# A fused transformer block on one core: the recurrence's projections token-major, merge blocks between its steps, modulation pieces spread

## The chip, the core and the metric

The kernel runs on one core of one Trainium2 chip. The metric is device time in microseconds (us) of one execution. Before the change three runs gave a median of 1801.65 us (1800.70 to 1803.32).

The engines are named as in the profile: PE is TensorE (matmuls; PEld its weight loads), ACT is ScalarE, DVE is VectorE, POOL is GpSimd and SP is SyncE, which issues the DMAs.

## What is computed

One block with 256 tokens (T) of width 2048 (D), batch 1, in fp32. Shapes and helpers are cut here to what the change touches:

```python
mod = silu(c) @ ada_w + ada_b                      # 2048 -> 6 x 2048: shifts, scales, gates
h = rmsnorm(x, norm1_g) * (1 + sc1) + sh1
z = h @ w_in                                       # 2048 -> 13360 columns
q, kc, vc, ks, vs, kw, vw, g_nsa, lx, ly, ga, gb = split(z)
o_a = nsa_attention(q, kc, vc, ks, vs, kw, vw, g_nsa, ...)   # 16 heads, 4 groups; kc, vc are compressed
u = causal_dwconv(lx, conv_w, conv_b)              # 4 taps over the tokens
r = sigmoid(blockdiag(u, w_a) + b_a);  i = sigmoid(blockdiag(u, w_i) + b_i)
log_a = 8 * r * log_sigmoid(lam)
hs = scan over tokens:  h_t = exp(log_a) h_(t-1) + sqrt(-expm1(2 log_a)) * (i * u)
o_b = gelu(ly) * hs
merged = sigmoid(ga) * (o_a @ proj_a) + sigmoid(gb) * (o_b @ proj_b)
x = x + g1 * (merged @ w_out)
h = rmsnorm(x, norm2_g) * (1 + sc2) + sh2
x = x + g2 * conv_glu_ffn(h, w_up, conv_w, conv_b, w_down)
return rmsnorm(x, final_g)
```

## The kernel before

**Weights and products.** Every weight matrix streams through once, in pieces of 1 MB (`stage`, L97: a tile `raw` of 128x2048, four buffers, loaded by SP's queue). A piece is worked on in two halves of 128x1024. `split` (L107, L108) makes of each half a rounded part `hi` by a copy on ScalarE and the rest `lo` by a subtraction on VectorE (three buffers each). The activations stand in the same two parts next to each other. A product takes three matmuls: hi by high part, hi by low part, lo by high part. All product outputs come from one pool of four PSUM banks (`bank`, name P).

**Two forms of product.** `dense_pair1` (L172 to L190) is feature-major: the weights are the stationary operand, 128 features come out on the partitions, and each matmul moves 256 columns (the tokens); one bank holds two feature tiles. `dense_tok` (L192 to L223) is token-major: the activations are stationary, 128 tokens come out on the partitions, and each matmul moves 512 columns (features); a block needs two banks, one for each half of the tokens. A half of weights is 12 matmuls in this form.

**Modulation pieces.** Most of `ada_w` does not pass through TensorE: `ada_piece` (L232 to L235) loads 1 MB and lets VectorE multiply and sum it into one column (L234). `filler(n)` (L487 to L493) runs the next n of 64 such pieces; the code calls it between blocks of other work. 48 pieces run ahead of the feed-forward network (FFN), the last 16 in it.

**Stages in order of time.** Norm, modulation and the input projection in four parts over the contraction (to about 230 us); its last part with the compression of kc and vc (`gather`, `compress`, to about 296 us); then eight attention units `attention(g, t)` woven into blocks of the input projection (L601 to L672). In the lx stage (L680 to L691) eight `dense_pair1` blocks give lx, with an attention unit and `filler(2)` behind each. The recurrence (L693 to L742) goes over four blocks `bt` of 512 features: the convolution on VectorE into u, two kinds of gate matmuls (banks lru_r and lru_i; the lru_i banks are those of attention's tp and oT), Sigmoid, Tanh, Exp and Sqrt on ScalarE, four scans on VectorE, then two `dense_pair1` blocks of ly whose GELU (L736) is written over u, times the scan's result, into oB (L740). ScalarE must load a table before a function of another set; `tbl(...)` keeps these functions in written order. The merge (L745 to L779) goes over four blocks n of 512 columns with two sides s (proj_a by oA, proj_b by oB): a gate block (n = 0 was computed earlier and lies in `mq`; its Sigmoid, L761, has been moved ahead into the attention), Sigmoid, product, multiply, add, transpose. Then the output projection and the FFN.

**What sets the order.** The kernel is written in the Tile framework. Each engine runs its instructions in one fixed order, which the framework's scheduler makes from the code by a model of the times; so an instruction can stand ahead of one that was written earlier, if nothing it needs is missing in the model. `high_priority` in `split` moves the hi and lo of the next weights ahead. Semaphores between engines keep the data right.

The recurrence's last step, L732 to L742, in short:

```python
for h in range(2):
    pl = dense_pair1([w_lru[8 + pr, k] for k in range(2)], h1r)
    tbl(A.activation(gl, pl..., AF.Gelu_apprx_tanh))
    V.tensor_tensor(gl, gl, iu[:, 2 * h:2 * h + 2], op=ALU.mult)
    ...
    filler(2 if pr % 4 == 0 else 0)
```

## Time and profile before

| | |
|---|---|
| Median of three runs | 1801.65 us |
| Profiled execution, its own time | 1802.45 us |
| Its span in the trace | 1800.3 us |
| PE busy | 1780.1 us, 99% |
| PEld busy | 1553.3 us, 86% |
| DVE busy | 1339.6 us, 74% |
| ACT busy | 871.5 us, 48% |
| POOL busy | 0.2 us |
| Mean granted clock of TensorE | 0.997 of full speed |
| Moved by DMA | 429.51 MB |

"Busy" is the union of an engine's instructions over the span. On TensorE instructions overlap, so their durations add up to more than the busy time; the distance of two starts in the timeline is what one costs. The idle time in front of an instruction is printed with what ended it: "[0.44 <-DVE lo L108]" is an engine that waited 0.44 us for a tile lo that VectorE wrote on line 108. "x8" at the end of a timeline row stands for eight equal instructions in a row.

### The profile page before, as it was taken

The page shows a single profiled execution, that of the slowest core. Times are in us where ns is not written, and L with a number is a line of the kernel's source. Part 1 is how long each engine was busy: PE and PEld are TensorE (multiplying, and loading weights), DVE is VectorE, ACT ScalarE, POOL GpSimd, SP SyncE. Part 2 cuts the span into 40 slices and gives each one's busy share as a digit, 9 for nine tenths or more (in the row PEclk, how much of TensorE's full clock was granted, in tenths as well). Part 3 has the DMA queues.
Part 4 walks back from the last instruction along what each step waited for, and adds up shares of the span by engine and source line. Part 5 has one row for each costly group of instructions (what it writes and reads, how often), then busy time and mean ns, then how long its engine had stood idle before and what let it go on. Part 6 is the DMA issues. An engine that isn't in the chain of part 4 may idle for free.

```text
span 1800.3 us, 25840 instructions
## 1 busy us (share of the span) xinstructions
PE 1780.1 (99%) x10336; PEld 1553.3 (86%) x10336; DVE 1339.6 (74%) x1955; ACT 871.5 (48%) x1185; POOL 0.2 (0%) x4
## 2 busy tenths in 40 slices
PE   8999999999999999999999999999999999999998
PEld 7899998888899888888888998888888888888886
DVE  7899875998788866767666898888555777766555
ACT  5654444655578443434445544444434444444443
POOL 0000000000000000000000000000000000000000
PEclk9999999999999999999999999999999999999999
DMA  9999863666556767777876566787755555555553
GB/s 348 359 333 365 317 231 129 211 214 228 211 179 223 276 239 295 285 288 286 291 274 206 177 234 235 279 283 282 252 190 189 189 192 192 192 190 190 187 192 112
DMA packets 64200, 429.51 MB, mean 239 GB/s; under 512 B 7088, under 2 KB 7376, under 8 KB 15568
## 3 DMA queue, kind: packets, MB, share of 16 engines
q1 hardware_dynamic: 63792, 427.08, 66.8%
q8 instruction: 81, 1.33, 0.3%
q10 hardware_dynamic: 288, 0.79, 0.1%
q14 instruction: 39, 0.32, 0.1%
HBM read 425.72 MB, written 2.11 MB: 238 GB/s over the span
## 4 chain that ended last, share of the span: by engine, by line
PE 94%; DVE 2%; ACT 2%; issue 1%; DMA 1%; DVEq 0%; ACTq 0%
PE P L130 26%; PE P L204 12%; PE P L205 12%; PE P L203 12%; PE P L187 3%; PE P L188 3%; PE P L185 3%; PE P L438 2%; PE P L440 2%; PE P L439 2%; PE P L432 1%; PE P L433 1%; PE P L431 1%; PE P L149 1%; PE P L148 1%; PE P L150 1%
## 5 line engine op out<-in xcount | busy, mean ns | idle before, releaser
L108 DVE TENSOR_TENSOR lo<-raw,hi 128x1024 fp32r<-128x1024 f32 x589 | 718.9, 1223 | 385.2 <-ACT hi L107 384.4
L107 ACT ACTIVATE hi<-raw 128x1024 fp32r<-128x1024 f32 x589 | 623.3, 1061 | 784.4 <-PE P L205 317.0
L130 PE MATMUL P<-h,hi 128*128 128x512 f32 x1344 | 463.9, 394 | 0.0
L130 PE MATMUL P<-h,lo 128*128 128x256 f32 x1344 | 366.4, 278 | 0.0
L130 PEld LDWEIGHTS P<-h,hi 128*128 128x128 f32 x1344 | 249.1, 188 | 54.9
L130 PEld LDWEIGHTS P<-h,lo 128*128 128x128 f32 x1344 | 252.4, 188 | 4.2
L234 DVE SCALAR_TENSOR_TENSOR raw<-raw,crow 128x2048 f32<-128x2048 f32 x64 | 146.4, 2287 | 4.7 <-DMA raw<-ada_w 4.5
L188 PE MATMUL P<-h,lo 128*128 128x256 f32 x512 | 147.7, 289 | 0.6 <-DVE lo L108 0.6
L187 PE MATMUL P<-h,hi 128*128 128x256 f32 x512 | 146.8, 287 | 0.0
L185 PE MATMUL P<-h,hi 128*128 128x256 f32 x512 | 146.7, 287 | 0.0
L438 PE MATMUL P<-h,hi 128*128 128x256 f32 x384 | 108.2, 286 | 0.0
L439 PE MATMUL P<-h,hi 128*128 128x256 f32 x384 | 107.5, 284 | 0.0
L440 PE MATMUL P<-h,lo 128*128 128x256 f32 x384 | 102.0, 283 | 0.0
L188 PEld LDWEIGHTS P<-h,lo 128*128 128x128 f32 x512 | 97.8, 191 | 1.7 <-DVE lo L108 1.4
L187 PEld LDWEIGHTS P<-h,hi 128*128 128x128 f32 x512 | 97.9, 191 | 1.4 <-issue 1.2
L185 PEld LDWEIGHTS P<-h,hi 128*128 128x128 f32 x512 | 97.9, 191 | 1.0 <-issue 0.7
L204 PE MATMUL P<-lo,ua 128*128 128x512 f32 x240 | 93.4, 389 | 0.0
L205 PE MATMUL P<-hi,ua 128*128 128x512 f32 x240 | 93.4, 389 | 0.0
L203 PE MATMUL P<-hi,ua 128*128 128x512 f32 x240 | 83.6, 389 | 0.0
L204 PE MATMUL P<-lo,h 128*128 128x512 f32 x192 | 75.3, 392 | 0.0
L205 PE MATMUL P<-hi,h 128*128 128x512 f32 x192 | 74.9, 390 | 0.0
L438 PEld LDWEIGHTS P<-h,hi 128*128 128x128 f32 x384 | 74.1, 193 | 0.2
(272 smaller groups left out, 3125.0 us busy)
## 6 DMA issues: line engine op xcount, KB each, us to landing
raw<-ada_w SPq DMA_DIRECT2D x96, 1024.0 KB, 5.0
raw<-w_up SPq DMA_DIRECT2D x96, 1024.0 KB, 4.9
raw<-w_down SPq DMA_DIRECT2D x48, 1024.0 KB, 4.9
raw<-w_lru SPq DMA_DIRECT2D x32, 1024.0 KB, 4.9
raw<-w_proj SPq DMA_DIRECT2D x32, 1024.0 KB, 5.0
raw<-w_gates SPq DMA_DIRECT2D x24, 1024.0 KB, 6.5
raw<-w_out SPq DMA_DIRECT2D x16, 1024.0 KB, 5.1
raw<-w_kv SPq DMA_DIRECT2D x24, 512.0 KB, 7.0
```

Of the source, the lines that this page charges most:

```text
L107: A.activation(hi[:, :n], raw[:, lo_col:lo_col + n], AF.Copy)
L108: V.tensor_tensor(lo[:, :n], raw[:, lo_col:lo_col + n], hi[:, :n].bitcast(F32), op=ALU.subtract)
L130: PE.matmul(ps[f][:, 0:256] if w else ps[f], hl[w][:, k * 256 + f * 128:k * 256 + f * 128 + 128], r[:, 0:256] if w else r, start=(kt == 0 ...
L185: PE.matmul(o, hi[:, sl], r[:, 0:256], start=(kt == 0 and f == 0), stop=False, skip_group_check=True)
L187: PE.matmul(o, hi[:, sl], r[:, 256:512], start=False, stop=False, skip_group_check=True)
L188: PE.matmul(o, lo[:, sl], r[:, 0:256], start=False, stop=(kt == n - 1), skip_group_check=True)
L203: PE.matmul(ps[j], xh, hi[:, w], start=(kt == 0), stop=False, skip_group_check=True)
L204: PE.matmul(ps[j], xh, lo[:, w], start=False, stop=False, skip_group_check=True)
L205: PE.matmul(ps[j], xl, hi[:, w], start=False, stop=(kt == n - 1), skip_group_check=True)
L234: V.scalar_tensor_tensor(raw, raw, 1.0, row, op0=ALU.mult, op1=ALU.mult, accum_out=modc[:, c:c + 1])
L438: PE.matmul(o, hi[:, sl], h1[:, kt, 0:256], start=first and f % 2 == 0, stop=False, skip_group_check=True)
L439: PE.matmul(o, hi[:, sl], h1[:, kt, 256:512], start=False, stop=False, skip_group_check=True)
```

## The change

1. **Token-major products for the recurrence.** `dense_pair1` goes. `w_lru` is packed in another layout, and the eight blocks of lx and ly (512 features each) are computed with `dense_tok`. Their output has tokens on the partitions and is turned by the new function `turned`: eight transposes on TensorE into two banks. For lx ScalarE copies the product out of PSUM, the transposes follow, and ScalarE copies them again. For ly the GELU writes the rows into u, the transposes follow, and VectorE multiplies straight from PSUM.
2. **Merge blocks between the steps of the recurrence.** `gates_of`, `open_gates` and `multiply` are the merge's parts as functions. Between the GELU of block bt and its transposes now stands a token-major block of the merge: the product of proj_a for n = 0 behind block 0, the gate block (1, 0) behind block 1, the product (1, 0) behind block 2, the gate block (1, 1) behind block 3. The Sigmoids of gates that wait (`mq` among them) stand in the next block's chain, ahead of its Exp.
3. **Modulation pieces spread.** `filler()` is now called behind each of the seven blocks of the input projection's last part; inside blocks, behind chosen pieces of weights (`fills`); and no longer in groups of two or four behind blocks of the merge. 48 pieces still run ahead of the FFN.
4. **Other slots.** The gathered compressed operands `gat` move from C2, C3 to C4, C5, `cmpb` from C7 to C3; the first of attention's p tiles moves from C3 to a tile xp, of which there is one buffer in place of two; two small tiles share one.

The diff, cut to what is named above:

```diff
-        def dense_pair1(pieces, rhs):
...
-        def dense_tok(pieces, lhs, late=None):
+        def dense_tok(pieces, lhs, late=None, fills=()):
...
+                if ip in fills:
+                    filler()
...
+        def turned(rows):
+            ps = [bank("turn"), bank("turn")]
+            for f in range(4):
+                for j in range(2):
+                    o = (f % 2) * 256 + j * 128
+                    PE.transpose(ps[f // 2][:, o:o + 128], rows[:, j, f * 128:f * 128 + 128], ident)
+            return [p.rearrange("p (f t) -> p f t", f=2) for p in ps]
...
-        gat = [big.tile([128, 16, 4, NCMP], F32, tag="C%d" % (2 + n), name="gat") for n in range(2)]
+        gat = [big.tile([128, 16, 4, NCMP], F32, tag="C%d" % (4 + n), name="gat") for n in range(2)]
...
         for i in range(4):
             whole(i, 3)
+            filler()
...
-        for pr in range(8):
-            pl = dense_pair1([w_lru[pr, k] for k in range(2)], h1r)
-            A.activation(lx[pr // 2][:, 2 * (pr % 2):2 * (pr % 2) + 2],
-                         pl.rearrange("p (f t) -> p f t", f=2), AF.Copy)
-            if units:
-                attention(*units.pop(0))
-            filler(2)
+        for bt in range(4):
+            ps = dense_tok([w_lru[bt, k] for k in range(4)], h1r, fills=(1, 3))
+            rows = lx[bt].rearrange("p (j a) t -> p j (a t)", j=2)
+            for j in range(2):
+                A.activation(rows[:, j], ps[j], AF.Copy)
+            for h, p in enumerate(turned(rows)):
+                A.activation(lx[bt][:, 2 * h:2 * h + 2], p, AF.Copy)
+            for _ in range(2):
+                if units:
+                    attention(*units.pop(0))
...
+        def gates_of(n, s):
+            if n == 0:
+                gated[n, s] = [mq[s][:, j] for j in range(2)]
+                return gated[n, s]
...
+            return dense_tok([w_gates[n - 1, s, k] for k in range(4)], h1r, fills=FILLS)
+
+        def open_gates(n, s, ps):
+            for j in range(2):
+                tbl(A.activation(gated[n, s][j], ps[j], AF.Sigmoid))
+
+        def multiply(n, s):
+            rhs = (lambda kt: oB[kt // 2][:, kt % 2]) if s else (lambda kt: oA[:, kt])
+            ps = dense_tok([w_proj[n, s, k] for k in range(4)], rhs, fills=(0, 1, 3) if s else FILLS)
+            for j in range(2):
+                V.tensor_tensor(gated[n, s][j], ps[j], gated[n, s][j], op=ALU.mult)
+
+        waiting = [(0, s, gates_of(0, s)) for s in range(2)]
...
+            while waiting:
+                open_gates(*waiting.pop(0))
             tbl(A.activation(r, r, AF.Exp, scale=-2.0))
...
-                pl = dense_pair1([w_lru[8 + pr, k] for k in range(2)], h1r)
+            ps = dense_tok([w_lru[4 + bt, k] for k in range(4)], h1r)
+            rows = u.rearrange("p (j a) t -> p j (a t)", j=2)
+            for j in range(2):
+                tbl(A.activation(rows[:, j], ps[j], AF.Gelu_apprx_tanh))
+
+            if bt % 2 == 0:
+                multiply(bt // 2, 0)
+            else:
+                waiting.append((1, bt // 2, gates_of(1, bt // 2)))
+            for h, p in enumerate(turned(rows)):
...
-                V.tensor_tensor(gl, gl, iu[:, 2 * h:2 * h + 2], op=ALU.mult)
+                V.tensor_tensor(gl, p, iu[:, 2 * h:2 * h + 2], op=ALU.mult)
```

**How instructions move.** On TensorE, behind the last attention unit's oT (L666), before: P is a product's bank, h_169 the activations, hi and lo the weights; product matmuls go on in this pattern.

```order
L188 MATMUL P<-h_169,lo 128x256
L666 MATMUL oT<-pT,vN 128x512 x4
L185 MATMUL P<-h_169,hi 128x256
L187 MATMUL P<-h_169,hi 128x256
L188 MATMUL P<-h_169,lo 128x256
```

The same place after (oT is now L660; the product on oA is that with proj_a):

```order
L186 MATMUL P<-hi,oA 128x512
L660 MATMUL oT<-pT,vN 128x512 x4
L736 MATMUL lru_i<-lt,raw 128x256 x2
L184 MATMUL P<-hi,oA 128x512
L185 MATMUL P<-lo,oA 128x512
L736 MATMUL lru_i<-lt,raw 128x256 x2
L186 MATMUL P<-hi,oA 128x512
```

And on TensorE eight matmuls of that product further on, again after:

```order
L186 MATMUL P<-hi,oA 128x512
L734 MATMUL lru_r<-lt,raw 128x256 x2
L736 MATMUL lru_i<-lt,raw 128x256 x2
L734 MATMUL lru_r<-lt,raw 128x256 x2
L736 MATMUL lru_i<-lt,raw 128x256 x2
L215 MATMUL turn<-cols,lt 128x128 x2
L184 MATMUL P<-hi,h_169 128x512
L185 MATMUL P<-lo,h_169 128x512
```

84 of the 96 matmuls of the product with proj_a stand ahead of the last oT; behind it come the other 12, the last four gate matmuls of block 0 and the eight of block 1, and the first two transposes (L215), which read the GELU of block 0. Behind these two stand 18 product matmuls of the next ly block, the other six transposes and 18 more product matmuls, on weights that are split by then. Before, 161 product matmuls stand between the last oT and the next block's first gate matmul on lru_r.

On ScalarE, the end of block 0's gate chain up to its first GELU (lt are the recurrence's tiles: r, iu, tt and u), before:

```order
L107 ACTIVATE hi<-raw 128x1024
L724 ACTIVATE lt<-lt 128x512
L725 ACT_TABLE_LOAD
L725 ACTIVATE lt<-lt 128x1024
L726 ACT_TABLE_LOAD
L726 ACTIVATE lt<-lt 128x1024
L107 ACTIVATE hi<-raw 128x1024 x2
L736 ACT_TABLE_LOAD
L736 ACTIVATE lt<-P 128x512
L107 ACTIVATE hi<-raw 128x1024 x2
L740 ACTIVATE oB<-lt 128x2x256
```

After:

```order
L107 ACTIVATE hi<-raw 128x1024
L744 ACTIVATE lt<-lt 128x512
L704 ACTIVATE mq<-mq 128x512 x4
L107 ACTIVATE hi<-raw 128x1024
L747 ACT_TABLE_LOAD
L747 ACTIVATE lt<-lt 128x1024
L748 ACT_TABLE_LOAD
L748 ACTIVATE lt<-lt 128x1024
L757 ACT_TABLE_LOAD
L757 ACTIVATE lt<-P 128x512 x2
L740 ACT_TABLE_LOAD
L740 ACTIVATE lt<-lru_r,cols 128x256
```

The Sigmoids on mq stand in the chain, and both GELUs (L757) stand between it and block 1's chain, which follows at once with no hi copy between.

## Rows read from the trace of the kernel before

**Rows 1.** The page's busy shares; one group of TensorE's by line (busy us, mean ns).
```profile
PE 1780.1 (99%) x10336; PEld 1553.3 (86%) x10336; DVE 1339.6 (74%) x1955; ACT 871.5 (48%) x1185; POOL 0.2 (0%) x4
...
L658 PE MATMUL tp<-cols,p 128*128 128x128 f32 x96 | 15.7, 272 | 0.5 <-ACT pcT L630 0.5
```

**Rows 2.** Busy time by stretch: from:to, length, each engine, clock, DMA share, GB/s.
```profile
231.00:296.00 65.00, 65.00 (x490) 60.58 (x489) 39.25 (x56) 22.76 (x26) 0.00 (x0) 1.00 0.49 178
...
425.00:480.00 55.00, 55.00 (x396) 48.23 (x396) 45.29 (x110) 31.75 (x74) 0.00 (x0) 1.00 0.60 212
480.00:594.00 114.00, 113.39 (x874) 109.19 (x873) 97.07 (x136) 85.68 (x113) 0.00 (x0) 1.00 0.58 205
594.00:900.00 306.00, 306.00 (x1362) 253.03 (x1361) 213.79 (x235) 129.24 (x144) 0.00 (x0) 1.00 0.78 283
```

**Rows 3.** Timeline, TensorE: start, us, line, tile; steps of 256 columns, transposes, a wait.
```profile
427.33 0.28 PE L185 MATMUL P<-h,hi 128*128 128x256 f32 x1
427.45 0.60 PE L658 MATMUL tp<-cols,p 128*128 128x128 f32 x4
427.80 0.36 PE L187 MATMUL P<-h,hi 128*128 128x256 f32 x1
428.00 0.28 PE L188 MATMUL P<-h,lo 128*128 128x256 f32 x1
...
561.36 0.39 PE L188 MATMUL P<-h,lo 128*128 128x256 f32 x1 [0.44 <-DVE lo L108]
```

**Rows 4.** Timeline, TensorE, a token-major product; twelve steps of 512 columns.
```profile
626.39 0.62 PE L203 MATMUL P<-hi,oB 128*128 128x512 f32 x2
...
629.11 0.62 PE L203 MATMUL P<-hi,oB 128*128 128x512 f32 x2
```

**Rows 5.** Timeline, TensorE, gate matmuls behind the last attention unit.
```profile
487.90 1.89 PE L716 MATMUL lru_i<-lt,raw 128*128 128x256 f32 x8
489.44 0.47 PE L185 MATMUL P<-h,hi 128*128 128x256 f32 x1
```

**Rows 6.** Timeline, ScalarE: the gate chains of blocks 0 and 1.
```profile
483.43 0.60 ACT L670 ACTIVATE oA<-oT 128x512 fp32r<-128x512 f32 x1 [3.58 <-PE oT L666]
485.10 1.06 ACT L107 ACTIVATE hi<-raw 128x1024 fp32r<-128x1024 f32 x1 [1.07 <-PE P L187]
487.98 1.06 ACT L107 ACTIVATE hi<-raw 128x1024 fp32r<-128x1024 f32 x1 [1.82 <-PE P L187]
488.94 0.58 ACT L685 ACTIVATE lx<-P 128x512 f32<-128x512 f32 x1
...
492.58 1.06 ACT L107 ACTIVATE hi<-raw 128x1024 fp32r<-128x1024 f32 x1 [1.96 <-PE P L187]
...
505.03 0.60 ACT L736 ACTIVATE lt<-P 128x512 f32<-128x512 f32 x1
...
515.21 1.28 ACT L720 ACT_TABLE_LOAD   x1
...
522.08 0.63 ACT L724 ACTIVATE lt<-lt 128x512 f32<-128x512 f32 x1 [0.56 <-DVE lt L722]
...
527.34 1.06 ACT L726 ACTIVATE lt<-lt 128x1024 f32<-128x1024 f32 x1
```

**Rows 7.** Timeline, ScalarE, in the attention: sigmoids on mq.
```profile
329.44 1.15 ACT L761 ACTIVATE mq<-mq 128x512 f32<-128x512 f32 x2
```

**Rows 8.** Timeline, VectorE: lo, scans; a modulation piece.
```profile
505.27 1.22 DVE L108 TENSOR_TENSOR lo<-raw,hi 128x1024 fp32r<-128x1024 f32 x1
506.40 2.43 DVE L731 TENSOR_TENSOR_SCAN lt<-lt 128x256 f32<-128x256 f32 x4
...
708.65 2.28 DVE L234 SCALAR_TENSOR_TENSOR raw<-raw,crow 128x2048 f32<-128x2048 f32 x1
```

**Rows 9.** Busy time by stretch, near the start of the span.
```profile
15.00:20.00 5.00, 3.96 (x31) 3.87 (x31) 4.47 (x6) 1.53 (x2) 0.00 (x0) 0.78 0.85 329
20.00:25.00 5.00, 4.32 (x22) 4.32 (x22) 4.42 (x5) 1.46 (x2) 0.00 (x0) 0.54 0.86 312
```

More of the change, by code (lines that the diff above doesn't have):

```diff
@@ L170, in up @@
             return take
-        def dense_pair1(pieces, rhs):
-            p = bank()
-            n = len(pieces) * 8
-            for ip, ap in enumerate(pieces):
-                raw = stage(ap)
-                for half in range(2):
-                    hi, lo = split(raw, half * 1024, 1024)
-                    for f in range(2):
-                        o = p[:, f * 256:f * 256 + 256]
-                        for k in range(4):
-                            kt = ip * 8 + half * 4 + k
-                            sl = slice(k * 256 + f * 128, k * 256 + f * 128 + 128)
-                            r = rhs(kt)
-                            PE.matmul(o, hi[:, sl], r[:, 0:256], start=(kt == 0 and f == 0), stop=False,
-                                      skip_group_check=True)
-                            PE.matmul(o, hi[:, sl], r[:, 256:512], start=False, stop=False, skip_group_check=True)
-                            PE.matmul(o, lo[:, sl], r[:, 0:256], start=False, stop=(kt == n - 1),
-                                      skip_group_check=True)
-            return p
-        def dense_tok(pieces, lhs, late=None):
+        def dense_tok(pieces, lhs, late=None, fills=()):
             ps = [bank(), bank()]
@@ L579, in block_kernel @@
             whole(8 + b, 3)
+            filler()
             if b == 0:
@@ L682, in block_kernel @@
             whole(10 + i, 3)
-        for pr in range(8):
-            pl = dense_pair1([w_lru[pr, k] for k in range(2)], h1r)
-            A.activation(lx[pr // 2][:, 2 * (pr % 2):2 * (pr % 2) + 2],
-                         pl.rearrange("p (f t) -> p f t", f=2), AF.Copy)
-            if units:
-                attention(*units.pop(0))
-            filler(2)
-        while units:
-            attention(*units.pop(0))
+        for bt in range(4):
[8 more added lines that the diff above has]
+                    attention(*units.pop(0))
+        assert not units
+        filler()
+        FILLS = (1, 3)
+        gated = {}
+        def gates_of(n, s):
+            if n == 0:
+                gated[n, s] = [mq[s][:, j] for j in range(2)]
+                return gated[n, s]
+            gated[n, s] = [tmp.tile([128, 512], F32, tag=(("r", "iu"), ("u", "tt"))[s][j], bufs=1, name="sg")
+                           for j in range(2)]
+            return dense_tok([w_gates[n - 1, s, k] for k in range(4)], h1r, fills=FILLS)
[8 more added lines that the diff above has]
+        waiting = [(0, s, gates_of(0, s)) for s in range(2)]
         oB = [None] * 8
@@ L741, in block_kernel @@
                 V.tensor_tensor(oB[pr][:, :, 256:512], gl, oh.bitcast(F32), op=ALU.subtract)
-                filler(2 if pr % 4 == 0 else 0)
+        while waiting:
+            open_gates(*waiting.pop(0))
         row1 = None
@@ L750, in block_kernel @@
         for n in range(4):
[L751 to L766 removed]
+            for s in range(2):
+                if (n, s) not in gated:
+                    open_gates(n, s, gates_of(n, s))
+                if s == 1 or n > 1:
+                    multiply(n, s)
+            m = [gated[n, s] for s in range(2)]
             if n == 2:
```

40 lines of the change are left out of this document (11 added, 29 removed).

## The prediction

> **What bounds the kernel now.** I read the busy shares first. TensorE is busy for 1780.1 of 1800.3 us; VectorE stands at 74%, ScalarE at 48% [rows 1]. The table of stretches says where that holds: from 425 to 480 us TensorE is busy 55.00 of 55.00, from 480 to 594 (the recurrence) 113.39 of 114.00, from 594 to 900 (merge and output projection) 306.00 of 306.00 [rows 2]. So in the stretch that is rewritten nothing but TensorE's own issue sets the time: a microsecond of issue saved is a microsecond gained, and a microsecond in which TensorE finds its next instruction not ready is lost for good, since nothing later has slack to give it back. To win there is little: 0.61 us of idle time between 425 and 900 us, perhaps 1.5 with the stretched starts around it. Durations on TensorE overlap (a transpose has a mean of 272 ns, [rows 1], yet four take 0.35 us from start to the next start, [rows 3]), so I price its instructions by the distance of starts in the timeline. The same instructions stand in both programs up to the last part of the input projection (231 us) and from the output projection on, so only that middle is costed.
>
> **Fewer, wider matmuls.** Sixteen pair products with 96 matmuls of 256 columns become eight token-major products with 96 of 512: 1536 become 768. At 256 columns a step is 427.45 - 427.33 = 0.120 us [rows 3]; at 512 columns twelve take 629.11 - 626.39 = 2.72 us, 0.227 each [rows 4]. 1536 x 0.120 = 184.3; 768 x 0.227 = 174.3: **-10.0 us**. The columns are the same number; only the fixed part of each matmul is saved.
>
> **Transposes.** Eight blocks x 8 = 64 transposes are new on TensorE. Four of them take 427.80 - 427.45 = 0.35 us, and the matmul behind them 0.20 instead of 0.12 (428.00 - 427.80) [rows 3], so 0.43 / 4 = 0.11 each: **+7.0 us**. Each lasts 0.272 on its own [rows 1]. The Trainium skill (TensorE: Matmul & The Clock Gate, Part 4: PE-mode transpose) gives about 275 ns for one; taken as the price of each, 64 would cost 17.6 us, by that page's figure an estimate, and the sum would be 10.6 us higher. The trace agrees with 275 as a duration, but not as a step: the four lie on top of each other.
>
> **ScalarE's extra copies and VectorE.** Eight copies of 128x512 are new on ScalarE, four table loads of 1.28 us go; both lie beside TensorE's work (ScalarE is busy 31.75 of 55.00 and 85.68 of 114.00 us, [rows 2]): nothing, as long as no matmul waits for them. VectorE's instructions are the same in number.
>
> **The hole at the first block of the recurrence.** This is the term that decides. TensorE takes its matmuls in the written order. The first two transposes of block 0 read the GELU of that block, and the GELU overwrites u, so it stands on ScalarE behind the whole gate chain of the block: sigmoids, Tanh, Exp, Sqrt and three table loads. The chain starts only when the last attention unit is through, because the input gates' banks lru_i are those of that unit's tp and oT. The block that should stand between, the product with proj_a, has been drawn ahead into the attention: 84 of its 96 matmuls stand before the last oT (the order, section on the change). Let T0 be the end of that oT.
>
> What TensorE still has after T0 until the first transpose: 12 matmuls of 512 columns (2.7 us) and 12 small ones of the gates, 8 of which took 489.44 - 487.90 = 1.54 us [rows 5] (so 2.3 at most); with the wait for the copy of oT (0.60, ScalarE's row at 483.43, [rows 6]) some 5.6 us.
>
> What ScalarE has until the first GELU is done: before, from the copy of oT at 483.43 to the end of the GELU at 505.63 it took 22.2 us [rows 6]. In it lie six hi copies (a step of 488.94 - 487.98 = 0.96 each: 5.8), one copy of lx (0.5) and three pauses of 1.07, 1.82 and 1.96 (4.9) that came from waiting for TensorE; without them 11.0. The new order adds in this place two hi copies (1.9) and four sigmoids on mq, 1.15 a pair [rows 7], 0.1 of it overlapped (2.1; before they stood in the attention). Sum 15.0. TensorE waits 15.0 - 5.6 = **+9.4 us**. Before, the same chain was covered: in the order of before 161 product matmuls of 256 columns, 19 us, stand between that oT and the next block's first gate matmul, and no product waits for the GELU but through its one bank of four.
>
> **The second wait, block 1's chain.** After the first transposes TensorE has 2 + 6 transposes (0.9) and 36 matmuls (8.2) on three halves of weights that are already split: 9.1 us. The fourth half's hi copy stands on ScalarE behind the second GELU and the whole gate chain of block 1. Before, such a chain took from the table load at 515.21 to the end of Sqrt, 528.40 [rows 6]: 13.2; without two hi copies and an oB copy that no longer stand there (2.6) and a pause of 0.56 10.0. The new one adds the GELU (0.5), the hi copy (1.0), the lo on VectorE that the second matmul needs (1.14, from 505.27 to 506.40, [rows 8]) and some 0.8, a third of the 2.4 us of four scans [rows 8] that stand on VectorE ahead of the scaling before the second Tanh. Sum 13.4, less 9.1 and the one matmul that needs no lo: **+4.1 us**.
>
> **VectorE behind it.** A half of weights keeps TensorE 12 x 0.227 = 2.72 us. Behind that wait VectorE has L729's work and two subtractions before the next lo (1.14 + 2 x 0.60 + 1.14 = 3.5), then four scans before the one after (2.4 + 1.14 = 3.5), later a modulation piece (2.28, [rows 8]) with conv steps, about 4.5 with its lo but eased by lighter halves ahead. 0.75 + 0.75 + 0.2: **+1.7 us**. Before, a place of this kind cost 0.44 us of idle time at 561.36 [rows 3].
>
> **The modulation pieces.** 48 of them still run before the FFN, 16 in it. Seven (7 x 2.28 = 16 us of VectorE, 7 MB) move into 231 to 296 us, where VectorE is busy 39.25 of 65.00 [rows 2]; the work fits, and weights are loaded two blocks ahead. They give nothing back where they came from: TensorE does not wait there. I take +0.5, between 0 (all hidden) and +3 (each of the seven delays one lo by the 0.44 seen at 561.36). The slots (C2, C3 to C4, C5; cmpb to C3; p to xp) move no instruction: 0. For the banks that turned() takes from the four of the products, I take +0.5 in all four lx blocks: attention work stands between the last matmul and the transposes.
>
> **The sum.** -10.0 + 7.0 + 9.4 + 4.1 + 1.7 + 0.5 + 0.5 = +13.2. The profiled execution took 1802.45 us (0.8 above the median of 1801.65): 1802.45 + 13.2 = 1815.7, less that 0.8: **1815 us**.
>
> **Rivals.**
> *TensorE's clock falls in the hole.* Early in the trace TensorE has gaps of about a us in five, and before them small work; the granted clock fell to a mean of 0.78 and 0.54 in 15 to 25 us, with the lower level of 1.2 GHz in part of each; TensorE was busy 3.96 and 4.32 of each 5.00 us there [rows 9]. A hole of 9.4 us would do the same. Two such rows lose 5 x 0.22 + 5 x 0.46 = 3.4 us. In my forecast the loss lies inside the second wait, where TensorE has 4.1 us to spare, so the sum stays; if that wait is shorter than I think, or the clock stays low until it ends, up to 3.4 come on top, and with the modulation pieces at their dearer end 1818 + 3 = 1821. [...]
> *Only the first hole.* If the fourth half comes in time, the second wait and the VectorE term go: 1815 - 5.8 = 1809; with the hole at 7 us, 1806.
> *No hole: not slower.* It needs the GELU done when TensorE reaches the transposes. That decides at 15.0 us of other TensorE work behind the last oT, against 5.6 in the order. Then only -10.0 + 7.0 and some 1.5 us of small waits (as at 561.36) remain: 1797 to 1799. For it: the kernel before hid the same chain fully. Against it: the order leaves nothing between, and an engine does not reorder its matmuls. That the change doesn't do what it says belongs here too: the transposes stand behind the block that follows in the code, but in block 0 that block is used up before.
> *The early pieces clog.* If VectorE, which takes its work in order, waits for the 1 MB loads of the pieces between 231 and 296 us (DMA share 0.49 there before, [rows 2]), each of the seven could hold a lo by a us: 1815 + 7 = 1822.
> *Transposes at their duration.* 64 x 0.272 = 17.4 instead of 7.0: 1825. Against it: the steps of 0.11 in [rows 3].
>
> **How the numbers follow.** Forecast (1809 to 1820) 0.66; clock 0.09; only the first hole 0.07; no hole 0.09; clogging 0.07; transposes 0.02. The range of 8 in 10 takes the forecast with its bounds, the first hole alone and most of the clock's case: 1805 to 1824. A difference under 0.2% (3.6 us) can't be told from none. Faster by more: 0.04 (the low end of "no hole"); within: 0.08 (its rest and the low end of the first hole alone); slower: 0.88.
>
> **What would show it.** In the trace of the changed kernel: about 8 to 10 us in which TensorE stands still ahead of the first turn on lt, released by the GELU on ScalarE; a second wait of 3 to 5 us for lo some 36 matmuls later; granted clock under 1 there; matmuls of w_lru 0.227 apart; no new wait after that. The prediction is wrong if TensorE is busy without a break from 425 to 600 us, if the transposes cost more than 0.11 each, or if waits show up between 231 and 425 us.

## The result, and the profile of the changed kernel

The changed kernel takes **1816.3 us** (median of four runs, 1815.13 to 1817.21) against 1801.18 us (1800.56 to 1803.32) for the kernel before: the ratio is 1.0081, with a 95% interval of 1.0069 to 1.0093. The prediction was 1815, with a range of 1805 to 1824. The execution profiled took 1815.99 us, its span is 1814.2 us; before it was 1802.45 and 1800.3.

The busy shares say little: TensorE is busy 4.5 us longer in a span that is 13.9 us longer, with 704 matmul records fewer. The second line is the group of the modulation pieces on VectorE; behind its busy time and mean stands the idle time ahead of it, here nearly ten times that of before.

```profile
PE 1784.6 (98%) x9632; PEld 1518.5 (84%) x9632; DVE 1344.1 (74%) x1955; ACT 871.3 (48%) x1189; POOL 0.2 (0%) x4
...
L227 DVE SCALAR_TENSOR_TENSOR raw<-raw,crow 128x2048 f32<-128x2048 f32 x64 | 146.5, 2289 | 42.7 <-DMA raw<-ada_w 42.4
```

The table of stretches (columns as in [rows 2]) has the place. From 535 to 543.3 us TensorE does almost nothing while ScalarE is busy 8.23 of 8.30 us; behind it TensorE is busy at a granted clock of 0.50 (the lower level, 1.2 GHz); and from 548.5 on it has the full clock and waits again. The first row is the stretch into which seven modulation pieces moved: TensorE is busy throughout.

```profile
231.00:295.00 64.00, 64.00 (x484) 59.55 (x483) 51.71 (x79) 22.25 (x26) 0.00 (x0) 1.00 0.78 305
535.00:543.30 8.30, 1.21 (x6) 0.73 (x4) 3.84 (x5) 8.23 (x10) 0.00 (x0) 0.69 0.71 256
543.30:548.50 5.20, 5.17 (x14) 4.11 (x15) 3.12 (x7) 5.11 (x11) 0.00 (x0) 0.50 0.01 5
548.50:560.00 11.50, 9.89 (x45) 7.58 (x44) 8.49 (x12) 9.53 (x12) 0.00 (x0) 1.00 0.11 38
```

TensorE's timeline through that place, with its waits in brackets, and two waits much later in the merge:

```profile
535.18 1.03 PE L736 MATMUL lru_i<-lt,raw 128*128 128x256 f32 x4
543.33 0.69 PE L215 MATMUL turn<-cols,lt 128*128 128x128 f32 x2 [7.12 <-ACT lt L757]
...
544.24 0.63 PE L185 MATMUL P<-lo,h 128*128 128x512 f32 x1
544.67 0.63 PE L186 MATMUL P<-hi,h 128*128 128x512 f32 x1
...
554.64 0.39 PE L186 MATMUL P<-hi,h 128*128 128x512 f32 x1
555.92 0.73 PE L184 MATMUL P<-hi,h 128*128 128x512 f32 x2 [0.90 <-ACT hi L107]
557.37 0.50 PE L185 MATMUL P<-lo,h 128*128 128x512 f32 x1 [0.72 <-DVE lo L108]
...
560.85 0.50 PE L185 MATMUL P<-lo,h 128*128 128x512 f32 x1 [0.45 <-DVE lo L108]
...
564.31 0.50 PE L185 MATMUL P<-lo,h 128*128 128x512 f32 x1 [0.45 <-DVE lo L108]
...
750.72 0.50 PE L185 MATMUL P<-lo,h 128*128 128x512 f32 x1 [0.53 <-DVE lo L108]
...
850.84 0.50 PE L185 MATMUL P<-lo,oA 128*128 128x512 f32 x1 [0.44 <-DVE lo L108]
```

The last gate matmul ends at 536.2; the transposes (turn) start at 543.33, released by the GELU (L757). Behind them steps of 512 columns are 544.67 - 544.24 = 0.43 us apart, twice the 0.227 of [rows 4].

ScalarE in the same time (its rows of before are [rows 6]): the copy of the last oT, the four sigmoids on mq, the last table load and the two GELUs, then at once block 1's chain, its Sqrt, and only then the fourth hi copy:

```profile
527.95 0.60 ACT L664 ACTIVATE oA<-oT 128x512 fp32r<-128x512 f32 x1 [3.52 <-PE oT L660]
...
533.50 2.19 ACT L704 ACTIVATE mq<-mq 128x512 f32<-128x512 f32 x4
...
541.38 1.28 ACT L757 ACT_TABLE_LOAD   x1
542.68 1.09 ACT L757 ACTIVATE lt<-P 128x512 f32<-128x512 f32 x2
543.78 1.28 ACT L740 ACT_TABLE_LOAD   x1
...
553.86 1.06 ACT L748 ACTIVATE lt<-lt 128x1024 f32<-128x1024 f32 x1
554.83 1.04 ACT L107 ACTIVATE hi<-raw 128x1024 fp32r<-128x1024 f32 x1
```

**Where the 13.9 us of span are.** The orders of TensorE agree up to 243.1 us (before) and 241.9 us (after, where a compression matmul comes next). From there to the first matmul of the output projection it is 658.3 us before and 673.9 after, +15.6; the start gives back 1.2 and what lies behind 0.5. I gave every matmul the median step of its tile and shape and added up what each took beyond it. The median steps sum to 652.7 and 649.6; the rest, late starts, is 5.6 and 24.3. (Where a wait is given "by starts" below, it is the distance of two starts less that median step.)

| | before | after | difference |
|---|---|---|---|
| median steps | 652.7 | 649.6 | -3.1 |
| late starts up to 525 us | 4.1 | 5.8 | +1.7 |
| to 554: after, the hole and the slow steps behind it | 0.4 | 10.2 | +9.8 |
| to 574: after, the second wait and VectorE behind it | 0.9 | 3.7 | +2.8 |
| from there to the output projection | 0.2 | 4.7 | +4.5 |

### The profile page after: what moved, and what is told of

It reads as the page before. It is cut to its first block, busy times and chain, and to the rows that moved or that the text cites. A ratio compares the mean times of both kernels' runs of the same rounds, so it can differ in the third digit from the quotient of the medians.

```text
span 1814.2 us, 24412 instructions
## 1 busy us (share of the span) xinstructions
PE 1784.6 (98%) x9632; PEld 1518.5 (84%) x9632; DVE 1344.1 (74%) x1955; ACT 871.3 (48%) x1189; POOL 0.2 (0%) x4
## 4 chain that ended last, share of the span: by engine, by line
PE 84%; DMA 7%; DVE 5%; ACT 2%; issue 2%; DVEq 0%; ACTq 0%
PE P L130 26%; PE P L185 12%; PE P L186 11%; PE P L184 11%; DMA raw<-ada_w 6%; PE P L432 2%; PE P L433 2%; PE P L434 2%; DVE raw L227 2%; PE P L426 2%; PE P L427 2%; PE P L425 1%; PE P L149 1%; PE P L148 1%; PE P L150 1%
## 5 line engine op out<-in xcount | busy, mean ns | idle before, releaser
L130 PE MATMUL P<-h,lo 128*128 128x256 f32 x1344 | 366.4, 278 | 0.0
L130 PEld LDWEIGHTS P<-h,hi 128*128 128x128 f32 x1344 | 249.1, 188 | 54.8
L130 PEld LDWEIGHTS P<-h,lo 128*128 128x128 f32 x1344 | 252.4, 188 | 4.2
L185 PE MATMUL P<-lo,h 128*128 128x512 f32 x448 | 179.9, 401 | 2.4 <-DVE lo L108 2.3
L227 DVE SCALAR_TENSOR_TENSOR raw<-raw,crow 128x2048 f32<-128x2048 f32 x64 | 146.5, 2289 | 42.7 <-DMA raw<-ada_w 42.4
L186 PE MATMUL P<-hi,h 128*128 128x512 f32 x448 | 176.5, 394 | 0.0
L184 PE MATMUL P<-hi,h 128*128 128x512 f32 x448 | 166.0, 397 | 0.9 <-ACT hi L107 0.9
L432 PE MATMUL P<-h,hi 128*128 128x256 f32 x384 | 108.2, 286 | 0.0
L433 PE MATMUL P<-h,hi 128*128 128x256 f32 x384 | 107.4, 284 | 0.0
L185 PEld LDWEIGHTS P<-lo,h 128*128 128x128 f32 x448 | 84.7, 189 | 23.2 <-DVE lo L108 6.0
L434 PE MATMUL P<-h,lo 128*128 128x256 f32 x384 | 101.8, 284 | 0.0
L184 PEld LDWEIGHTS P<-hi,h 128*128 128x128 f32 x448 | 84.7, 189 | 18.5 <-ACT hi L107 1.3
L186 PEld LDWEIGHTS P<-hi,h 128*128 128x128 f32 x448 | 84.8, 189 | 17.1 <-issue 0.7
L432 PEld LDWEIGHTS P<-h,hi 128*128 128x128 f32 x384 | 74.2, 193 | 0.2
L433 PEld LDWEIGHTS P<-h,hi 128*128 128x128 f32 x384 | 74.2, 193 | 0.0
L316 DVE SCALAR_TENSOR_TENSOR raw<-raw,crow 128x2048 f32<-128x2048 f32 x31 | 70.7, 2284 | 2.4 <-DMA raw<-ada_w 2.3
```

What stands on the lines that cost most here:

```text
L130: PE.matmul(ps[f][:, 0:256] if w else ps[f], hl[w][:, k * 256 + f * 128:k * 256 + f * 128 + 128], r[:, 0:256] if w else r, start=(kt == 0 ...
L184: PE.matmul(ps[j], xh, hi[:, w], start=(kt == 0), stop=False, skip_group_check=True)
L185: PE.matmul(ps[j], xh, lo[:, w], start=False, stop=False, skip_group_check=True)
L186: PE.matmul(ps[j], xl, hi[:, w], start=False, stop=(kt == n - 1), skip_group_check=True)
L227: V.scalar_tensor_tensor(raw, raw, 1.0, row, op0=ALU.mult, op1=ALU.mult, accum_out=modc[:, c:c + 1])
L316: V.scalar_tensor_tensor(raw, raw, 1.0, crow, op0=ALU.mult, op1=ALU.mult, accum_out=mc)
```

## The experiments

Times are medians, with lowest and highest in parentheses; ratios are to the kernel before, run on the same chip, with the 95% interval.

**1. Sigmoids of mq back in the attention.** Edit against the changed kernel:

```diff
-        waiting = [(0, s, gates_of(0, s)) for s in range(2)]
+        waiting = []
+        for s in range(2):
+            for j, g in enumerate(gates_of(0, s)):
+                A.activation(g, g, AF.Sigmoid)
```

> The changed kernel, with the four Sigmoids on mq no longer tied into block 0's gate chain (they are free to run in the attention, as before the change). Theory (TensorE waits for the GELU behind the gate chain of block 0): the chain is 2.1 us shorter (four Sigmoids, 533.50 to 535.58 in the trace of after), the hole falls from 7.3 to about 5.1 us, the second wait behind it stays: 1816.3 - 2.1 = about 1814. Rival 'form' (token-major products and transposes cost the time) and rival 'pieces' (the spread modulation pieces do): no change, 1816.

Measured: 1815.33 us (1812.52 to 1818.99), 1.0074 [1.0054, 1.0093]. TensorE's row at the transposes:

```profile
541.35 0.69 PE L215 MATMUL turn<-cols,lt 128*128 128x128 f32 x2 [5.04 <-ACT lt L760]
```

The hole shrinks from 7.12 to 5.04 us, by 2.1, what the four sigmoids take: the length of ScalarE's chain sets it. But the second wait becomes 1.50 + 0.71 and two waits in the merge 0.77 and 0.81, and the total can't be told from that of the changed kernel.

**2. Block 0's transposes behind the next ly block.** `finish` holds what stood behind the merge block (transposes, product, oB); for block 0 it is now called behind ly of block 1:

```diff
             ps = dense_tok([w_lru[4 + bt, k] for k in range(4)], h1r)
+            while later:
+                finish(*later.pop(0))
...
+            later.append((bt, u, iu, rows))
+            if bt not in (0,):
+                finish(*later.pop(0))
```

> The changed kernel, with block 0's transposes and what follows on them behind the product of block 1's ly; in TensorE's order 36 of that product's matmuls (8.2 us) then stand between the gate matmuls and the first transpose. Theory: the hole falls from 7.3 to under 1 us, the granted clock stays at 1.00 (2.2 us of doubled steps go) and the second wait (1.1 + 0.9 us) goes or halves; the two VectorE waits of 0.7 each stay: 1816.3 - 11 = about 1805 (1803 to 1807). Rivals 'form' and 'pieces': all matmuls, transposes and pieces are still there, so 1816.

Measured: 1812.76 us (1811.56 to 1815.78), 1.0061 [1.0046, 1.0076]. A miss: the hole went and only some 3.5 us came back. TensorE's timeline, then the stretches from 540 to 550 us:

```profile
544.66 1.03 PE L215 MATMUL turn<-cols,lt 128*128 128x128 f32 x8
...
548.11 0.73 PE L184 MATMUL P<-hi,h 128*128 128x512 f32 x2 [2.42 <-ACT hi L107]
...
550.65 0.80 PE L185 MATMUL P<-lo,h 128*128 128x512 f32 x1 [1.80 <-DVE lo L108]
```

```profile
540.00:545.00 5.00, 5.00 (x26) 4.13 (x25) 2.45 (x2) 4.94 (x6) 0.00 (x0) 1.00 0.38 156
545.00:550.00 5.00, 1.43 (x9) 0.75 (x7) 3.57 (x7) 4.99 (x10) 0.00 (x0) 0.93 0.00 0
```

The transposes wait for nothing now. TensorE runs through ly of block 1 instead and then stands before the next weights, whose hi copies are in ScalarE's queue behind block 0's chain and the start of block 1's; ScalarE is busy 4.94 and 4.99 of each 5.00 us. The wait moved to the next thing that ScalarE owes.

**3. Modulation pieces where the kernel before calls them.** The changed kernel without `filler()` in the input projection and without `fills`, with `filler(2)` behind attention units and the first half of a recurrence step of blocks 0 and 2, `filler(2)` or `filler(4)` behind a product:

```diff
-            ps = dense_tok([w_proj[n, s, k] for k in range(4)], rhs, fills=(0, 1, 3) if s else FILLS)
+            ps = dense_tok([w_proj[n, s, k] for k in range(4)], rhs, fills=())
...
+            filler(2 if n == 0 else 4)
```

> The changed kernel, with the modulation pieces called where the kernel before called them: none in the last part of the input projection, two behind each attention unit of the lx stage, two behind recurrence blocks 0 and 2, two or four behind each product of the merge. Theory, with the addition that the trace of after suggests: VectorE's 42.4 us of waiting for the pieces' loads fall to some 5 us, and with them TensorE's small waits for lo behind 570 us (0.69 at 749.8, 0.60 at 850.0, 0.50 at 720.9 and smaller, some 4 us together); hole and second wait stay: 1812 to 1813. Rival 'pieces': the spread is the whole loss, 1801. If the pieces cost nothing: 1816.

Measured: 1826.56 us (1825.71 to 1827.35), 1.0135 [1.012, 1.015]. A miss by 14 us. Stretches, then TensorE and ScalarE at the largest wait behind the second one (the hole, 7.60 us, and the second wait, by now 2.24 + 2.02, are still there):

```profile
560.00:700.00 140.00, 132.78 (x571) 106.80 (x572) 103.38 (x136) 76.10 (x91) 0.00 (x0) 0.96 0.60 218
700.00:926.00 226.00, 226.00 (x1007) 186.34 (x1006) 161.51 (x184) 97.54 (x112) 0.00 (x0) 1.00 0.76 285
```

```profile
658.53 1.11 PE L184 MATMUL P<-hi,h 128*128 128x512 f32 x2 [2.91 <-ACT hi L107]
```

```profile
657.42 2.00 ACT L107 ACTIVATE hi<-raw 128x1024 fp32r<-128x1024 f32 x2 [2.40 <-DMA raw<-w_lru]
```

Behind a product is now inside the recurrence, since products (0, 0) and (1, 0) have moved there; the groups of pieces stand in VectorE's and the loads' way, and the next weights come 2.40 us late. In the merge no wait is left: 226.00 of 226.00. So the small waits of the merge in the changed kernel go when the pieces stand elsewhere, but calling them as before is no undoing, because the places have moved.

**4. Both together (2 and 3).**

> Both edits of the two runs before together. Theory: what is left of the change is -3 us (fewer, wider matmuls less the transposes) and the two or three VectorE waits of the recurrence (about 2 us): 1800 to 1802, level with the kernel before. Rival 'form': 1812 or more.

Measured: 1816.7 us (1815.89 to 1818.54), 1.0082 [1.0067, 1.0097]. A miss for the same two reasons: TensorE waits 2.39 and 4.02 us at 547 and 552, and 1.50 and 2.62 at 640 and 649.

**5. The kernel before with lx token-major alone.**

```diff
-        for pr in range(8):
-            pl = dense_pair1([w_lru[pr, k] for k in range(2)], h1r)
...
+        for bt in range(4):
+            ps = dense_tok([w_lru[bt * 2 + k // 2, k % 2] for k in range(4)], h1r)
...
+            for h, p in enumerate(turned(rows)):
+                A.activation(lx[bt][:, 2 * h:2 * h + 2], p, AF.Copy)
```

> The kernel before, with the four lx blocks alone token-major (and transposed, copied twice); attention units, modulation pieces, slots, recurrence and merge stay as before. Theory: 768 matmuls of 256 columns become 384 of 512, -5.0 us, 32 transposes +3.5, small waits +0.3: 1801.5 - 1.2 = about 1800, no loss. Rival 'form' (the token-major form with its transposes is what costs): half of the loss of 15 us, 1807 or more.

Measured: 1822.57 us (1820.53 to 1823.24), 1.012 [1.0103, 1.0136]. A miss, and the largest: half of the change costs more than all of it. The stretches, then ScalarE and TensorE at the largest wait:

```profile
465.00:490.00 25.00, 19.13 (x72) 10.62 (x72) 21.26 (x70) 14.97 (x42) 0.00 (x0) 0.90 0.35 127
530.00:540.00 10.00, 5.08 (x35) 4.88 (x34) 10.00 (x20) 8.68 (x10) 0.00 (x0) 0.81 0.40 147
```

```profile
535.77 1.06 ACT L740 ACTIVATE lt<-lt 128x1024 f32<-128x1024 f32 x1
536.74 1.99 ACT L107 ACTIVATE hi<-raw 128x1024 fp32r<-128x1024 f32 x2
```

```profile
537.83 0.58 PE L185 MATMUL P<-h,hi 128*128 128x256 f32 x1 [4.92 <-ACT hi L107]
```

With lx alone the last attention units have too little beside them (19.13 of 25.00 us) where before TensorE was full [rows 2], and a chain on ScalarE delays a hi copy by 4.92 us. The trace shows where the time is; why the scheduler's order came out so is open. It says this much: summed as in the table above, the median steps are 1.6 us less than before (1.5 by the forecast of this run) and the late starts 27.8 against 5.6, so the cost is not in the form of the products but in what stands between them.

**6. Each transposition of lx four times.**

```diff
-                    PE.transpose(ps[f // 2][:, o:o + 128], rows[:, j, f * 128:f * 128 + 128], ident)
+                    for _ in range(times):
+                        PE.transpose(ps[f // 2][:, o:o + 128], rows[:, j, f * 128:f * 128 + 128], ident)
```

> The changed kernel, with each of the 32 transposes of the lx stage issued four times over (the same result, 96 transposes more). Theory (a transposition costs its step of 0.11): 1816.3 + 96 x 0.108 = about 1827. Rival (it costs its duration of 0.272): 1816.3 + 26 = 1842. If they hid beside other work: 1816.

Measured: 1820.46 us (1819.56 to 1821.62), 1.0107 [1.0092, 1.0122]. The total is a miss and answers nothing by itself, since the order moved as well: the 7 us ahead of the transposes are gone and the largest wait is 2.83 us at 550.60. Summed as in the table above, the median steps are 10.4 us more than in the changed kernel, as the theory has it, and the late starts 6.2 less. The rows:

```profile
367.57 1.09 PE L216 MATMUL turn<-cols,lx 128*128 128x128 f32 x8
368.42 0.48 PE L184 MATMUL P<-hi,h 128*128 128x512 f32 x1
```

Eight take 368.42 - 367.57 = 0.85 us, 0.106 each; all 128 of lx come to 13.6 us by their starts, at a mean duration of 0.273 each (34.9 if added up). The Trainium skill (TensorE: Matmul & The Clock Gate, Part 4: PE-mode transpose) gives about 275 ns; as a duration that agrees with the 0.273 here, as a price it is 2.6 times the step of 0.106.

**7. The hole filled with idle matmuls.** Thirty matmuls into two banks of the products' pool, read by nobody, behind the product of block 0:

```diff
+                if bt == 0:
+                    for p in (bank("idle"), bank("idle")):
+                        for k in range(15):
+                            PE.matmul(p, h1[:, k, 0:128], h1[:, k], start=(k == 0), stop=(k == 14), skip_group_check=True)
```

> The changed kernel, with 30 matmuls of 512 columns into two banks that nobody reads, put behind the product with proj_a, so that TensorE is busy for some 6.8 us of the 7.3 us hole. Theory (the loss by the low clock lies inside the second wait, which ScalarE sets): the granted clock stays at 1.00 behind the hole and the steps of 0.43 us become 0.23, but TensorE then waits 2 us longer for the fourth half's hi: 1816 (within 1 us). Rival (the low clock is a loss of its own): 1814 or less.

Measured: 1821.86 us (1821.06 to 1827.7), 1.0121 [1.0103, 1.0139]. The stretches of the hole and of what was slow behind it, then TensorE and ScalarE:

```profile
535.00:543.30 8.30, 8.30 (x39) 6.96 (x38) 3.87 (x5) 8.24 (x9) 0.00 (x0) 1.00 0.73 272
543.30:548.50 5.20, 4.84 (x25) 3.64 (x24) 3.09 (x6) 5.10 (x11) 0.00 (x0) 1.00 0.00 0
```

```profile
558.24 1.22 PE L184 MATMUL P<-hi,h 128*128 128x512 f32 x2 [4.53 <-ACT hi L107]
...
560.87 0.79 PE L185 MATMUL P<-lo,h 128*128 128x512 f32 x1 [1.41 <-DVE lo L108]
```

```profile
557.14 2.93 ACT L107 ACTIVATE hi<-raw 128x1024 fp32r<-128x1024 f32 x3
```

A miss: the total is 5.6 us above that of the changed kernel, where none was expected. The clock stays at 1.00 and nothing is gained: TensorE is sooner through its matmuls and waits longer for the same hi copy. That copy also comes 557.14 - 554.83 = 2.3 us later, as two copies of oB got into the chain. By starts the two waits grow from 1.06 + 0.89 to 4.70 + 1.81; without these 2.3 us they are 4.2, as much as low clock (2.2) and second wait (1.95) together in the changed kernel. By that the low clock was no loss of its own. The order changed with the edit, so in this run it rests on one subtraction. The changed kernel's own trace agrees: between its GELUs and the late hi copy at 554.83 ScalarE waits once, 0.76 us at 549.56, and that for VectorE and not for TensorE, so faster matmuls would not have brought the copy sooner.

**8. Pieces out of the recurrence's products and lx blocks.** `FILLS = ()`, `filler(2)` behind attention units, `filler(4)` behind the products of the merge proper:

```diff
-        FILLS = (1, 3)
+        FILLS = ()
...
+            if s == 1 or n > 1:
+                filler(4)
```

> The changed kernel with its seven early pieces, but none between the blocks of the recurrence: 17 in the lx stage, 24 behind the six products of the merge that follow the recurrence, in groups of four as in the kernel before. Theory now (pieces among the recurrence's work, and pieces whose loads VectorE waits for in the merge, cost TensorE some 4 us of waits for lo; grouped pieces cost only where merge products stand in the recurrence, as the run with the pieces as before showed): hole and second wait stay, 1811 to 1813. Rival (any grouping costs, the spread is a gain): 1818 or more.

Measured: 1816.51 us (1816.12 to 1816.83), 1.0085 [1.007, 1.01]; a miss, no gain. VectorE's waits for the pieces' loads fall to 5.9 us (waits by line: total, times, longest), but TensorE's waits stay: 7.11 at the transposes, 0.62, 0.72, 0.46 and 0.41 behind them, 0.41 at 607.83, 0.72 at 660.29, 1.03 at 740.57. Ahead of that last one VectorE worked off three pieces between 728.29 and 737.93, 2.28 us each and none waiting for its load, before it came to the lo: here it is the time that pieces in a group take which held TensorE, and not a late load.

```profile
DVE raw L227 <- DMA raw<-ada_w: 5.9, 7, 1.8
```

**9. The product with proj_a written ahead of the recurrence.** In the code it stood behind block 0's GELU and was drawn ahead by the scheduler; here it is written where most of it ran. In this kernel the product is multiplied by mq before mq's Sigmoid, so this part of the merge computes something else, by the same instructions.

```diff
         waiting = [(0, s, gates_of(0, s)) for s in range(2)]
+        multiply(0, 0)
...
-            if bt % 2 == 0:
-                multiply(bt // 2, 0)
-            else:
+            if bt == 2:
+                multiply(1, 0)
+            elif bt % 2:
```

> The changed kernel with one call moved: the product with proj_a for n = 0 is written ahead of block 0 of the recurrence instead of behind its GELU. It is then what the attention draws on, and ly's first block, which needs nothing of the attention, is left to stand behind the last oT: in TensorE's order 85 product matmuls of 512 columns (19 us) then stand between that oT and the first transpose, against 12 in the changed kernel. All matmuls, transposes and pieces are the same in number. Theory (the hole is a gate chain of ScalarE without cover): hole (7.3), low clock (2.2) and most of the second wait (2.2) go, some small waits of VectorE stay: 1816.3 - 10 = about 1806 (1804 to 1809). Rival 'moved' (the wait goes to another place, as in the run with the transposes later): 1812. Rival 'form': 1816.

Measured: 1809.64 us (1807.99 to 1814.03), 1.0052 [1.0039, 1.0065], an interval apart from that of the changed kernel. TensorE at the transposes, and the stretch ahead of them:

```profile
537.43 0.40 PE L186 MATMUL P<-hi,h 128*128 128x512 f32 x1
537.67 0.38 PE L215 MATMUL turn<-cols,lt 128*128 128x128 f32 x2
```

```profile
528.00:536.00 8.00, 7.87 (x35) 6.30 (x34) 3.19 (x3) 7.95 (x9) 0.00 (x0) 1.00 0.20 83
```

One call moved, the same instructions, 6.7 us less by the medians. The transposes wait for nothing and the clock stays up: other products now stand between the last oT and the transposes. It is 3.6 us short of the forecast and 0.6 outside its range: some is given back earlier, 1.51 us at 496.90 and 0.71 at 508.47, and waits for lo stay behind the transposes, 0.71 at 540.38, 0.72 at 555.33 and 1.18 at 568.71.

**10. The recurrence rewritten by hand.** Gate matmuls, chain, ly, GELU and transposes as functions, in an order that gives TensorE work under each chain; pieces only in merge products and later gate blocks:

```diff
+        multiply(0, 0)
+        ly(0)
+        gatesmm(0)
+        chain(0)
+        gatesmm(1)
+        ly(1)
+        gelu(0)
+        finish(0)
+        chain(1)
...
```

> The changed kernel with all its parts in another order: the product with proj_a first, the ly block of block 1 ahead of block 0's GELU, the transposes of a block behind the next block's ly, the merge's gate blocks and second product late in the recurrence, the Sigmoids on mq free to run in the attention, no modulation pieces inside the recurrence (they go into the merge blocks behind it). Same matmuls, same 64 transposes, same 48 pieces. Theory: no hole, no second wait, full clock, some 2 us of small waits left, and the -3 us of fewer, wider matmuls less transposes: 1801 to 1804, level with the kernel before. Rival 'form': the form itself costs more than was worked out, 1806 or more.

Measured: 1806.78 us (1804.8 to 1811.0), 1.0035 [1.0023, 1.0047]. The best order of the change that computes the same, and still slower than the kernel before. It misses the theory's 1801 to 1804, and the time alone falls to the rival 'form'; the trace does not: the median steps sum to 649.6 as in the changed kernel, 3.1 less than before, and late starts are 15.6 against 5.6. The recurrence, the merge, and VectorE's waits for pieces:

```profile
528.00:560.00 32.00, 30.23 (x134) 23.72 (x133) 24.19 (x30) 26.22 (x34) 0.00 (x0) 1.00 0.42 155
700.00:906.00 206.00, 203.61 (x902) 166.33 (x901) 163.14 (x191) 86.93 (x101) 0.00 (x0) 1.00 0.88 326
```

```profile
DVE raw L227 <- DMA raw<-ada_w: 41.4, 29, 4.6
```

**11. The kernel before with the other slots alone** (gat, cmpb, p and the small tiles as in the change).

```diff
-        gat = [big.tile([128, 16, 4, NCMP], F32, tag="C%d" % (2 + n), name="gat") for n in range(2)]
+        gat = [big.tile([128, 16, 4, NCMP], F32, tag="C%d" % (4 + n), name="gat") for n in range(2)]
```

> The kernel before with the moved slots alone (the gathered operands in C4 and C5, cmpb in C3, the first p and the two small tiles in one buffer of xp). Theory: no instruction moves on any engine and no wait appears: 1801, no difference within 0.2%. Rival (the single buffer of xp makes the four heads of an attention unit wait for each other): slower by 2 us or more.

Measured: 1801.42 us (1799.95 to 1802.69), 1.0001 [0.9992, 1.001]. No difference in time, though in the profiled execution TensorE has three waits for lo in the merge (0.27, 0.53 and 0.43 us at 680.32, 724.68 and 769.99) where before it had none.

**12. The order of 10, pieces without their loads.**

```diff
+                    raw = wpool.tile([128, 2048], F32, tag="raw", bufs=4, name="raw")
+                    V.scalar_tensor_tensor(raw, crow, 1.0, crow, op0=ALU.mult, op1=ALU.mult, accum_out=modc[:, c:c + 1])
```

> The run 'reordered' with the modulation pieces of the merge and the FFN left without their loads: VectorE does the same 128x2048 multiply and sum on a tile that is there already, so that part of the modulation is not computed; the order of TensorE's work in the recurrence stays. Theory (TensorE's small waits for lo in the merge, five of 0.5 to 0.84 us between 808 and 901 us, come from VectorE standing in front of a piece whose load has not landed): they go, 1806.8 - 3.4 = about 1803.5. Rival (they come from the 2.3 us that a piece keeps VectorE busy): 1807.

Measured: 1804.91 us (1803.35 to 1807.21), 1.0023 [1.0014, 1.0032]. VectorE's waits for pieces and the merge:

```profile
DVE raw L227 <- DMA raw<-ada_w: 13.1, 8, 4.2
```

```profile
700.00:903.00 203.00, 203.00 (x908) 167.99 (x907) 161.13 (x189) 87.10 (x102) 0.00 (x0) 1.00 0.55 195
```

The pieces' arithmetic is still there, their loads mostly not, and the merge has no wait left (203.00 of 203.00 against 203.61 of 206.00): in that order the waits of the merge come from pieces whose loads have not landed, not from their 2.3 us of VectorE. On the median that is 1.9 us, with intervals that overlap; the rows of the merge carry the verdict, not the total.

## Why the prediction was right, point by point

**Form, -10.0 + 7.0.** The median steps give -3.1 us against -3.0. A transposition costs 0.106 on its own too, eight in a row in run 6, as forecast from four; the rival "transposes at their duration" is out.

**The hole, 9.4.** It measured 7.12, under the 8 to 10 us that I named as its sign. The mechanism was right: the place, the releaser (the GELU) and the reason. ScalarE's chain was forecast at 15.0 us and took 15.3 (from 527.95 to the first GELU's end, 543.28). Run 1 takes four sigmoids out and the hole shrinks by just their time. That the block meant as cover is drawn ahead is what run 9 tells: with the product out of the way in the code, other products take its place and the hole is gone. The term that was mis-sized is TensorE's cover: 5.6 forecast, 8.3 measured (536.2 - 527.95). I priced 12 gate matmuls at 1.54 us for eight [rows 5], but those eight are records, and a gate matmul has two: the 12 appear as 24, four of which take 0.85 us (528.60 - 527.75 in TensorE's timeline), 5.1 in all and not 2.3.

**The second wait, 4.1, and the clock.** By starts the wait measured 1.06 + 0.89 = 1.95 us. The missing 2.2 is the low clock: 11 steps that start from 543.67 to 548.08 took 0.427 (the first 0.57) in place of 0.227. Together 4.15. The rival "clock falls" was half right: the clock did fall, to 0.50, but the loss lay inside the wait, as the forecast had it, and run 7 agrees. For that rival [rows 9] were weak ground: the granted clock was down to 0.50 at 18.0 to 18.5 us already, while TensorE ran matmuls of one column without a break, and its one gap of 1.72 us came behind these. The fall in an idle stretch is what the changed kernel shows. The Trainium skill (TensorE: Matmul & The Clock Gate, Why this matters for your kernels) asks for no idle gaps between bursts. Its rule held here: the granted clock in the stretch behind the hole is 0.50. But filling the gap gave no time back, since ScalarE set the end.

**VectorE behind it, 1.7.** By starts 0.62 + 0.61 = 1.2 us at 560.85 and 564.31.

**The modulation pieces, +0.5, and "no new wait after that".** This step failed. Where I had looked, between 231 and 295 us, nothing is lost. But 4.5 us are lost between 574 us and the output projection, where I had none. Seven waits of 0.15 to 0.69 us (by starts, the longest at 750.72) make 2.7 of them; the rest is some two dozen late starts of 0.2 or less. The seven have two causes. Three, at 721.46, 750.72 and 850.84, 1.8 us together, are the pieces': before the lo for which TensorE waits, VectorE stood in front of a piece whose load had not landed, as here:

```profile
747.22 2.29 DVE L227 SCALAR_TENSOR_TENSOR raw<-raw,crow 128x2048 f32<-128x2048 f32 x1 [2.05 <-DMA raw<-ada_w]
...
749.44 1.22 DVE L108 TENSOR_TENSOR lo<-raw,hi 128x1024 fp32r<-128x1024 f32 x1
```

In the whole span it did so for 42.4 us in 33 waits, where before it was 4.5 us in 8. That was my rival "the early pieces clog" in another place: I asked whether a load would be late where the pieces were added, and not where they were spread to. The merge's waits go when the loads go (run 12, in another order); in the changed kernel itself taking pieces out of the recurrence only moved them (run 8). The other four waits, at 607.46, 613.19, 659.35 and 665.08, 0.9 us together, have no piece ahead of them: there VectorE waits 4.0 us for the Sqrt of the gate chains of blocks 2 and 3 (at 605.04 and 656.93) and then runs scaling and scans ahead of the next lo. That is the term "VectorE behind it", which I had counted for block 1 alone. Which of the two the small late starts belong to is not shown.

**Banks and the attention, +0.5.** Late starts up to 525 us, where the last oT ends, grew by 1.7; what they are stays open.

**The slots, 0.** Run 11 confirms it.

**The sum.** The total came out as near as 1 us partly by luck, because two misses cancel: the hole was 2.3 us smaller than forecast, and the late starts behind 574 us were 4.5 larger; the start of the span and what lies behind the merge took back 1.7.

**What stays open.** Run 10 has no hole and full clock and is still 5.4 us slower than the kernel before. In its trace are 0.98 us at 493.40, three waits of 0.71, 0.46 and 0.60 between 552 and 560, and those of the merge; by starts, late ones up to 525 us are some 3 larger than before. Without the pieces' loads some 4 us remain (ratio 1.0023). Whether an order without these exists was not tried.

## What to carry to other kernels

On engines that run in order, a block of work covers a chain only if it still stands behind the chain's start when the scheduler is done: count, in the order as it will run and not as it is written, what each engine has between the last input and the first instruction that needs the result, and write first the block that the scheduler would draw ahead anyway, so that another is left to stand behind the start of the chain (run 9). When one engine owes two results in a row, taking away the wait for the first moves it to the second; look at what it serves next before pricing the gain. Spreading loads over an in-order engine that also feeds the critical one can trade few long queues for many places where it stands before data not yet there (here 42.4 us in 33 waits, 4.5 in 8 before); in groups it is the pieces' arithmetic that stands ahead of the next lo (run 8).

## What the runs showed of the hardware

- An fp32 matmul of the gates with 256 columns leaves two records in the trace and takes about 0.43 us for both (0.85 for two matmuls); a product of fp32r with 512 columns leaves one and takes 0.227. Counting records of one as instructions of the other halves the price.
- Behind a gap of 7.1 us the granted clock was 0.50 although TensorE was fully busy, then 1.00 again; 11 steps were nearly doubled (2.2 us), and by the subtraction of run 7 the kernel lost nothing by it, because the next weights were later still.
